# Hybrid RWKV-7 / latent-attention layer on one core: 188 intermediate stores issued by the POOL queue instead of the SP queue

## The chip, the core and the metric

The kernel runs on one core of one Trainium2 chip. A core has TensorE (PE, matrix products; PEld is its weight load), VectorE (DVE), ScalarE (ACT), GpSimd (POOL) and SyncE (SP), each with its own instruction stream that runs in order, and 16 DMA engines that move data between the chip's memory (DRAM) and the on-chip buffer. A DMA is issued by one of the streams: when its turn comes there and its semaphores are met, it is handed to the DMA engines, and the stream goes on. An instruction that waits holds everything behind it in the same stream.

The metric is device time in microseconds. The kernel before ran at a median of 2458.2 us over 3 runs (2451.07 to 2459.61).

## The reference

One decoder layer over 2048 tokens of width 1024. All is float32; the kernel makes each product out of three products of a high and a low part, so every weight is split into two.

```python
u = rmsnorm(h, g_pre)
proj = u @ w_in                                  # 1024 x 5152
feat_a, z_a, c_q, c_kv, k_pe, z_b, gate_logits = split_cols(proj, ...)
f = feat + mu_shift * (prev - feat)              # token shift of r, k, v, wd, ad (1664 columns)
...                                              # branch A: RWKV-7 recurrence over f, group norm, silu(z_a), w_out_a
...                                              # branch B: attention from the latents c_q, c_kv, silu(z_b), w_out_b
gates = sigmoid(gate_logits + b_gate)
merged = g_a * y_a + g_b * y_b
h = h + rmsnorm(merged @ w_o, g_post)
```

## The kernel before, in words

The tokens are cut into four segments of 512 (`NS = 4`), the columns of `w_in` into tiles of 128. There are three phases: projections with the recurrence of branch A (to about 1125 us), attention (to about 1760 us), and the gates, merge and output projection (to the end).

**Projection.** For each column tile `proj` runs 24 matmuls (8 blocks of the contraction, three products each). Its weights come from `load_w` in two halves of four blocks. The first time, a half is loaded raw (`wraw`, two buffers), split by ACT (high part, L247) and POOL (low part, L248) into `whl` (three buffers), and, where the tile is wanted later, stored to DRAM as `d_wi` (L273). Every later time `whl` is loaded ready from `d_wi` (L265). In segment 0 half of the tiles are stored, in segment 1 the other half; in `gates_seg` all 24 tiles are.

**Features.** `proj_seg` shifts r, k, v and the low-rank inputs (`shift`: ACT L328, DVE L330 and L331, a POOL copy of the last column into `halo` at L332) and stores them as `d_k`, `d_r`, `d_v`, `d_wa`; the three latent tiles go out as `d_lat`. `elem` reads these back in halves of a segment (`kf`, `rf`, `vf`, `wat`, and `cum`, `Pi`, `u` for the latents); for segment 0 it does so at once, for the others one to two steps later. `gates_seg` makes 42 tiles of gate factors for the last two segments and stores them as `d_zg`, to be read in the third phase.

**Recurrence.** `step` works on blocks of 256 tokens: `zblock` builds `Zr` and stores it to `d_q`; `gather` reads it back as `Qg` and `Xg`; `invert` runs 30 short DVE steps and stores and reloads the result (`Xinv`); `merge`, `chunk` and `gnorm` follow. These DMAs are on SP (half of the gather on ACT).

**Order.** The program is handed to a scheduler that simulates the engines and puts each engine's instructions, DMA issues among them, in the order of its simulated times. A change of a DMA's queue therefore moves other instructions as well. From the second phase's start on most of the order is fixed by hand (`pin`).

Stores and loads of the first phase are all issued by SP, apart from the loads of `X` from `d_x`, the stores of `d_cq`, `d_kv`, `d_kr` (POOL) and half of the gather (ACT).

Of the kernel before, what the change touches and what calls it, by code (L numbers as in the profile page):

```python
# [21 lines left out]
KC = D // P  # L22
# [18 lines left out]
def f32(ap):  # L41
    return ap.bitcast(F32)
# [7 lines left out]
def hybrid_layer(ctx, tc, x, positions, g_pre, w_in, b_gate, mu_shift, w0, w_decay_up, a0, w_iclr_up, k_k, k_a,  # L50
                 r_k, gn_gain, gn_bias, w_out_a, g_q, w_uq, g_kv, w_ukv, w_out_b, w_o, g_post, out):
    nc = tc.nc
    V, A, G, PE = nc.vector, nc.scalar, nc.gpsimd, nc.tensor
# [14 lines left out]
    sa = pst.enter_context(tc.tile_pool(name="p1a", bufs=1, reuse_waits="tile"))  # L68
# [85 lines left out]
    for name, ap in (("mu", mu_shift), ("w0", w0), ("a0", a0), ("kk", k_k), ("ka", k_a), ("rk", r_k), ("gg", gn_gain),  # L154
                     ("gb", gn_bias), ("gq", g_q), ("gkv", g_kv), ("bg", b_gate)):
        n = ap.shape[0] // P
# [15 lines left out]
    def dcol(o, i=0):  # L172
        return dv[:, o + i:o + i + 1]

    def parameters():

        prow = pp.tile([P, 512], F32, name="prow", tag="z", bufs=2)
        PE.transpose(prow[:, :NR], rows[:NR, :], ident[:NR, :NR])
        A.copy(prm, prow[:, :NR])
        G.tensor_scalar(dv[:, OMU:OMU + 13], cols("mu", 13), -1.0, 1.0, op0=ALU.mult, op1=ALU.add)  # L180
        G.tensor_scalar(dv[:, HW0:HW0 + 4], cols("w0", 4), 0.5, None, op0=ALU.mult)
        G.tensor_scalar(dv[:, HA0:HA0 + 4], cols("a0", 4), 0.5, None, op0=ALU.mult)
        G.tensor_scalar(dv[:, HKA:HKA + 4], cols("ka", 4), 0.5, None, op0=ALU.mult)
        G.tensor_scalar(dv[:, OKA:OKA + 4], cols("ka", 4), -0.5, 1.0, op0=ALU.mult, op1=ALU.add)
        G.tensor_scalar(dv[:, HBG:HBG + 16], cols("bg", 16), 0.5, None, op0=ALU.mult)


    def dtile(name, shape, dt=F32):
        return dr.tile(shape, dt, name=name)

    d_f = {(n, p, s): dtile(f"d_{n}{p}_{s}", [P, 512]) for n in "krv" for p in range(NP) for s in range(NS)}
# [6 lines left out]
    d_wa = {s: dtile(f"d_wa{s}", [P, 512]) for s in range(NS)}  # L198
# [4 lines left out]
    d_zg = {(s, i): dtile(f"d_zg{s}_{i}", [P, 512]) for s, n in ((NS - 1, 24), (NS - 2, 18)) for i in range(n)}  # L203
    d_lat = {(i, s): dtile(f"d_lat{i}_{s}", [P, 512]) for i in range(3) for s in range(NS)}
# [41 lines left out]
    def split(hi, lo, src, ehi, elo):  # L246
        (ehi.copy if ehi is A else ehi.tensor_copy)(hi, src)  # L247
        elo.tensor_tensor(lo, src, f32(hi), op=ALU.subtract)  # L248


    d_w = {}

    def load_w(pool, src, nk, n, elo=None, bufs=3, tag="w", pieces=None, raws=2, key=None, keep=True):


        res = []
        kept = d_w.get(key)
        if key is not None and kept is None and keep:
            d_w[key] = dtile(f"d_w{key}", [P, -(-nk // 4), 2, 4, n])
        for k0 in range(0, nk, 4):  # L260
            m = min(4, nk - k0)
            w = pool.tile([P, 2, m, P], F32R, name=f"{tag}hl", tag=f"{tag}hl", bufs=bufs)
            wn = w if n == P else w[:, :, :, 0:n]
            if kept is not None:
                nc.sync.dma_start(f32(wn), kept[:, k0 // 4])  # L265
            else:
                raw = pool.tile([P, m, P], F32, name=f"{tag}raw", tag=f"{tag}raw", bufs=raws)
                for lo_, n_, ap in (pieces or [(0, n, src)]):
                    nc.sync.dma_start(raw[:, :, lo_:lo_ + n_],
                                      ap[k0 * P:(k0 + m) * P, :].rearrange("(c p) n -> p c n", p=P))  # L270
                split(wn[:, 0], wn[:, 1], raw[:, :, 0:n], A, elo or G)
                if key is not None and keep:
                    nc.sync.dma_start(d_w[key][:, k0 // 4], f32(wn))  # L273
            res += [(w[:, 0, c, 0:n], w[:, 1, c, 0:n]) for c in range(m)]
        return res

# [8 lines left out]
    def proj(ps, w, X, cut=1, mm=PE.matmul):  # L285

        XH, XL = X
        for i in range(cut):
            t = slice(i * 512 // cut, (i + 1) * 512 // cut)
            mm3(ps[:, t], [(w[c], (XH[:, c, t], XL[:, c, t])) for c in range(KC)], mm=mm)  # L290
# [11 lines left out]
    with st:  # L302
# [30 lines left out]
            return f  # L333

        def wtile(c0, n=P, elo=None, keep=True):
            return load_w(sa, w_in[:, c0:c0 + n], KC, n, elo, key=f"i{c0}", keep=keep)

        def pj():
            return ppa.tile([P, 512], F32, name="pj", tag="pj", bufs=2)

        X = [sa.tile([P, KC, 512], F32R, name=n) for n in ("xh", "xl")]
# [87 lines left out]
        def proj_seg(s):  # L429
            make_xT(sa, ppa, "pj", 2, s, g_rep, X)  # L430
            if s == 0:
                parameters()
            cols_ = slice(s * 512, (s + 1) * 512)

            def later(i):

                return bool(s or i % 2)


            ps = pj()  # L440
            proj(ps, wtile(1536, elo=G if s else V, keep=later(0)), X, 2)
            f = shift(ps, 12)
            A.activation(f[0:HD, :], f[0:HD, :], AF.Tanh)
            nc.sync.dma_start(d_wa[s], f)
            yield
            for p in range(NP):
                ps = pj()
                proj(ps, wtile(512 + p * P, keep=later(p)), X)
                f = shift(ps, 4 + p)
                nc.sync.dma_start(d_f["k", p, s], f)  # L450
                yield
            for i, c0 in enumerate((C_CQ, C_CQ + P, C_CKV)):
                ps = pj()
                proj(ps, wtile(c0, keep=later(i)), X)
                f = sa.tile([P, 512], F32, name="lat", tag="fsh", bufs=2)
                A.copy(f, ps)
                nc.sync.dma_start(d_lat[i, s], f)
                yield

            for p in range(NP):  # L460
                for nm, c0, j in (("r", 0, 0), ("v", 1024, 8)):
                    ps = pj()
                    proj(ps, wtile(c0 + p * P, keep=later(j // 8)), X)
                    f = shift(ps, j + p)
                    nc.sync.dma_start(d_f[nm, p, s], f)
                    yield

            ps = pj()
            k1 = w_in[:, C_KPE:C_KPE + 32]
            proj(ps[0:HD, :], load_w(sa, None, KC, HD, pieces=[(0, 32, k1), (32, 16, k1[:, 16:32]),  # L470
                                                               (48, 16, k1[:, 0:16])], key="kpe"), X)
            rt = sa.tile([P, 512], F32, name="rtab", tag="mf", bufs=2)
            nc.sync.dma_start(rt[0:HD], d_rope[32:96, cols_])
            ra = sa.tile([P, 512], F32, name="ra", tag="fsh", bufs=2)
            rb = sa.tile([P, 512], F32, name="rb", tag="fsh", bufs=2)
            V.tensor_tensor(ra[0:32], ps[0:32, :], rt[0:32, :], op=ALU.mult)
            V.tensor_tensor(rb[0:32], ps[32:64, :], rt[32:64, :], op=ALU.mult)
            G.tensor_tensor(ra[0:32], ra[0:32], rb[0:32], op=ALU.add)
            kr = [sa.tile([P, 512], F32R, name=f"kr{k}", tag="mf", bufs=2) for k in range(2)]
            split(kr[0][0:32], kr[1][0:32], ra[0:32], G, G)  # L480
            for k in range(2):
                G.dma_start(d_kr[:, k, cols_], kr[k][0:32])
            yield

        def gates_seg():

            xs = NS - 1
            for s, i in d_zg:
                if s != xs:
                    xs = s  # L490
                    load_xT(X, s)
                ps = pj()
                c0 = (C_ZA, C_ZB, C_G, C_G + 4 * P, C_G + 8 * P, C_G + 12 * P)[i // 4] + (i % 4) * P
                proj(ps, wtile(c0), X)
                th = sa.tile([P, 512], F32, name="thg", tag="mf", bufs=2)
                if i < 8:
                    A.activation(th, ps, AF.Tanh, scale=0.5)
                    V.scalar_tensor_tensor(th, th, 1.0, ps, op0=ALU.add, op1=ALU.mult)
                else:
                    A.activation(th, ps, AF.Tanh, scale=0.5, bias=dcol(HBG, i - 8))  # L500
                nc.sync.dma_start(d_zg[s, i], th)
                yield

        def uv_new():
# [589 lines left out]
    with ExitStack() as st:  # L1094
# [165 lines left out]
        for i in range(NG):  # L1260
# [9 lines left out]
            if i == NG - NS - 1:  # L1270
# [6 lines left out]
                X = [sx.tile([P, KC, 512], F32R, name=n) for n in ("xh3", "xl3")]  # L1277
# [3 lines left out]
        for p in range(4):  # L1281
            if p < 3:
                ps = pp.tile([P, 2, 512], F32, name="pj2", tag="st", bufs=3)[:, 0]
                proj(ps, load_w(sx, w_in[:, C_ZA + p * P:C_ZA + (p + 1) * P], KC, P, elo=V, bufs=5,
                                key=f"i{C_ZA + p * P}"), X, mm=pin)
                th = sx.tile([P, 512], F32, name=f"th0{p}")
# [7 lines left out]
    with ExitStack() as st:  # L1294
# [16 lines left out]
        for si, s in enumerate(order):  # L1311
# [3 lines left out]
            for br, c0, dsrc in ((0, C_ZA, d_ya), (1, C_ZB, d_ob)):  # L1315
                BH = sb.tile([P, NP, 512], F32R, name=f"BH{br}", tag=f"BH{br}", bufs=1)
                BL = sb.tile([P, NP, 512], F32R, name=f"BL{br}", tag=f"BL{br}", bufs=1)
                for p in range(NP):
                    y = t_("yin")
                    nc.sync.dma_start(y, dsrc[p, s])  # L1320
                    th = t_("th3") if s or br or p >= len(gates0) else gates0[p]
# [4 lines left out]
                    else:  # L1326
                        ps = pj()
                        proj(ps, load_w(sx, w_in[:, c0 + p * P:c0 + (p + 1) * P], KC, P, elo=V, bufs=5,
                                        key=f"i{c0 + p * P}"), X)
# [7 lines left out]
            for m in range(KC):  # L1337
                prods = []
                for br, wsrc in ((0, w_out_a), (1, w_out_b)):
# [3 lines left out]
                    else:  # L1343
                        ps = pj()
                        c0 = C_G + br * D + m * P
# [81 lines left out]
```

## Time and profile before

| | before |
|---|---|
| median of 3 runs | 2458.2 us |
| profiled execution | 2459.4 us |
| its span, first to last instruction | 2457.7 us |
| PE / DVE / ACT / POOL busy | 2216.5 / 1099.8 / 710.4 / 1020.3 us |
| DMA moved | 455 MB, 185 GB/s over the span |
| mean granted TensorE clock | 0.950 of full speed |

The span is cut at 145 us (end of segment 0's projections), 720 us (end of segment 3's), 950 us (last weight store), 1125 us (start of the attention phase). The tables of waits name the waiting engine and line, the releaser, the total, the number of waits and the longest. SPq stands for the issues of the SP stream.

### The profile page before, as it was taken

What the parts mean: (1) busy time and instruction counts of PE and PEld (TensorE: products, weight loads), DVE (VectorE), ACT (ScalarE), POOL (GpSimd) and SP (SyncE); (2) the same over time, 40 slices, a digit from 0 to 9 for tenths busy, and PEclk for the clock granted to TensorE, in tenths of its full rate; (3) what the DMA queues carried; (4) which work ended last, traced back from release to release, by engine and by line L of the source; (5) the groups of instructions that cost most, each with busy time, mean ns of one, the idle gap of its engine ahead of it and who ended that gap; (6) DMA issues with size and microseconds to landing.
All of it is one profiled execution on the core that took longest, in us unless ns stands there. A gap on an engine that the chain in (4) does not pass through costs nothing.

```text
span 2457.7 us, 37858 instructions
## 1 busy us (share of the span) xinstructions
PE 2216.5 (90%) x14313; PEld 1646.5 (67%) x14313; DVE 1099.8 (45%) x2007; ACT 710.4 (29%) x1283; POOL 1020.3 (42%) x1194
## 2 busy tenths in 40 slices
PE   7978988988989897998698998988999989999997
PEld 5656776767766675776465655555678867788876
DVE  7155675667475847434353435344230231300312
ACT  4343342333324342123233333332321211111111
POOL 6474443445254655222245653555533232312422
PEclk9989989989999998999699999999999999999999
DMA  7777866647657787574211112050297895766863
GB/s 252 217 251 236 242 211 185 191 125 222 178 174 230 233 239 239 170 230 128 72 58 57 49 59 76 29 189 7 82 371 232 282 325 197 283 204 199 318 245 120
DMA packets 315182, 455.15 MB, mean 185 GB/s; under 512 B 114044, under 2 KB 207288, under 8 KB 309368
## 3 DMA queue, kind: packets, MB, share of 16 engines
q1 hardware_dynamic: 285112, 406.06, 51.3%
q0 software_dynamic: 12608, 42.47, 5.2%
q10 hardware_dynamic: 17280, 4.20, 1.0%
q8 instruction: 113, 1.85, 0.3%
q14 instruction: 69, 0.57, 0.1%
HBM read 313.69 MB, written 132.64 MB: 182 GB/s over the span
## 4 chain that ended last, share of the span: by engine, by line
PE 54%; DMA 18%; DVE 17%; POOL 3%; issue 3%; ACT 2%; SPq 2%; ACTq 0%; DVEq 0%; POOLq 0%
PE pj L281 7%; PE pst L294 7%; PE pj L282 7%; PE pj L283 7%; PE po L294 5%; DMA wraw<-in_w_in_dram 3%; DMA whl<-d_wi 3%; DVE mx L1049 3%; DMA Xg<-d_q 2%; DVE Xg L698 2%; DVE tq L696 2%; PE py L281 2%; PE py L283 2%; PE py L282 2%; PE pq L294 2%
## 5 line engine op out<-in xcount | busy, mean ns | idle before, releaser
L281 PE MATMUL pj<-xh,whl 128*128 128x512 f32 (+1 forms) x1320 | 536.4, 406 | 46.3 <-DMA whl<-d_wi 27.1
L283 PE MATMUL pj<-xh,whl 128*128 128x512 f32 (+1 forms) x1320 | 531.9, 403 | 10.0 <-POOL whl L248 9.7
L282 PE MATMUL pj<-xl,whl 128*128 128x512 f32 (+1 forms) x1320 | 529.9, 401 | 0.0
L1172 POOL TENSOR_TENSOR acc<-acc,pt 128x1024 f32<-128x1024 f32 (+2 forms) x144 | 290.5, 2017 | 204.7 <-PE po L294 177.4
L281 PEld LDWEIGHTS pj<-xh,whl 128*128 128x128 f32 x1320 | 256.2, 194 | 116.6 <-DMA whl<-d_wi 29.6
L283 PEld LDWEIGHTS pj<-xh,whl 128*128 128x128 f32 x1320 | 256.1, 194 | 74.1 <-POOL whl L248 15.3
L282 PEld LDWEIGHTS pj<-xl,whl 128*128 128x128 f32 x1320 | 256.4, 194 | 55.6 <-issue 2.5
L1049 DVE TENSOR_REDUCE mx<-pm 128x2 f32<-128x1024 f32 (+3 forms) x160 | 164.4, 1060 | 148.1 <-PE pm L294 147.4
L248 POOL TENSOR_TENSOR whl<-wraw,whl 128x512 fp32r<-128x512 f32 (+1 forms) x114 | 147.4, 1294 | 160.9 <-ACT whl L247 155.8
L1352 DVE SCALAR_TENSOR_TENSOR tg<-tg,py 128x512 f32<-128x512 f32 x64 | 43.9, 687 | 306.0 <-PE py L283 207.1
L1159 ACT ACTIVATE pt<-pst 128x1024 f32<-128x1024 f32 (+2 forms) x144 | 125.2, 883 | 163.5 <-PE pst L294 150.4
L1354 POOL TENSOR_TENSOR tg<-tg 128x512 f32<-128x512 f32 x32 | 41.2, 1288 | 211.7 <-DVE tg L1352 211.7
L247 ACT CAST whl<-wraw 128x512 fp32r<-128x512 f32 (+1 forms) x116 | 71.1, 615 | 179.4 <-DMA wraw<-in_w_in_dram 106.1
L294 PE MATMUL po<-pt,Vt 128*64 128x512 f32 (+3 forms) x576 | 121.4, 538 | 0.0
L281 PE MATMUL py<-BH,whl 128*128 128x512 f32 x256 | 103.2, 404 | 10.2 <-DMA whl<-d_wo 5.2
L294 PE MATMUL pm<-KH,QH 64*128 64x512 f32 (+3 forms) x312 | 71.6, 447 | 40.5 <-DVE mx L1049 34.8
L282 PE MATMUL py<-BL,whl 128*128 128x512 f32 x256 | 102.8, 402 | 0.0
L283 PE MATMUL py<-BH,whl 128*128 128x512 f32 x256 | 102.6, 402 | 0.0
L696 DVE TENSOR_TENSOR tq<-Xg,Qg 128x30 f32<-128x30 f32 (+7 forms) x240 | 84.8, 353 | 38.4 <-DMA Xg<-d_q 33.0
L282 PE MATMUL pout<-wf,MH 128*128 128x512 f32 x256 | 101.1, 395 | 0.0
L283 PE MATMUL pout<-wf,ML 128*128 128x512 f32 x256 | 99.5, 395 | 0.0
L281 PE MATMUL pout<-wf,MH 128*128 128x512 f32 x256 | 97.3, 395 | 0.1
(368 smaller groups left out, 3953.1 us busy)
## 6 DMA issues: line engine op xcount, KB each, us to landing
whl<-d_wi SPq DMA_DIRECT2D x222, 512.0 KB
d_wi<-whl SPq DMA_DIRECT2D x80, 512.0 KB
wraw<-in_w_in_dram SPq DMA_DIRECT2D x98, 256.0 KB
whl<-d_wo SPq DMA_DIRECT2D x48, 512.0 KB
wf<-d_wf SPq DMA_DIRECT2D x48, 512.0 KB
cqt<-d_cq POOLq DMA_DIRECT2D x16, 1024.0 KB, 5.5
d_zg<-thg SPq DMA_DIRECT2D x42, 256.0 KB
xl<-d_x POOLq DMA_DIRECT2D x8, 1024.0 KB, 9.9
```

Source lines behind the costliest of these rows:

```text
L247: (ehi.copy if ehi is A else ehi.tensor_copy)(hi, src)
L248: elo.tensor_tensor(lo, src, f32(hi), op=ALU.subtract)
L281: mm(ps, lhsT=lh, rhs=rh, start=(i == 0), stop=False)
L282: mm(ps, lhsT=lh, rhs=rl, start=False, stop=False)
L283: mm(ps, lhsT=ll, rhs=rh, start=False, stop=(stop and i == n - 1))
L294: tc.keep_in_program_order(PE.matmul(*args, **kw))
L696: V.tensor_tensor(t3, Xg[:, 0:m, s_:s_ + 1].to_broadcast([P, m, n]), Qg[:, s_:s_ + 1, s_ + 1:32].to_broadcast([P, m, n]), op=ALU.mult)
L698: V.tensor_tensor(Xg[:, 0:m, s_ + 1:32], Xg[:, 0:m, s_ + 1:32], t3, op=ALU.add)
L1049: V.tensor_reduce(mx[:, :, j, c], pm[:, :, 0:w], axis=AX.X, op=ALU.max)
L1159: A.activation(pt[:, :, q0:512], pst[:, :, q0:512], AF.Exp, scale=scale)
L1172: G.tensor_tensor(acc[:, :, q0:512], acc[:, :, q0:512], pt[:, :, q0:512], op=ALU.add)
L1352: V.scalar_tensor_tensor(tg, tg, 1.0, po, op0=ALU.add, op1=ALU.mult)
```

## The change

The 188 stores of the first phase go to POOL's stream: 80 of `d_wi`, 2 of `d_wkpe`, 52 of shifted features, 12 of latents, 42 of gate factors. `load_w` gets an argument `out_q`; its callers in the attention phase and the third phase don't pass it and keep SP. No size, buffer or arithmetic changes.

```diff
-    def load_w(pool, src, nk, n, elo=None, bufs=3, tag="w", pieces=None, raws=2, key=None, keep=True):
+    def load_w(pool, src, nk, n, elo=None, bufs=3, tag="w", pieces=None, raws=2, key=None, keep=True,
+               out_q=None):
...
                 if key is not None and keep:
-                    nc.sync.dma_start(d_w[key][:, k0 // 4], f32(wn))
+                    (out_q or nc.sync).dma_start(d_w[key][:, k0 // 4], f32(wn))
...
         def wtile(c0, n=P, elo=None, keep=True):
-            return load_w(sa, w_in[:, c0:c0 + n], KC, n, elo, key=f"i{c0}", keep=keep)
+            return load_w(sa, w_in[:, c0:c0 + n], KC, n, elo, key=f"i{c0}", keep=keep, out_q=G)
...
-            nc.sync.dma_start(d_wa[s], f)
+            G.dma_start(d_wa[s], f)
...
-                nc.sync.dma_start(d_f["k", p, s], f)
+                G.dma_start(d_f["k", p, s], f)
...
-                nc.sync.dma_start(d_lat[i, s], f)
+                G.dma_start(d_lat[i, s], f)
...
-                    nc.sync.dma_start(d_f[nm, p, s], f)
+                    G.dma_start(d_f[nm, p, s], f)
...
-                                                               (48, 16, k1[:, 0:16])], key="kpe"), X)
+                                                               (48, 16, k1[:, 0:16])], key="kpe", out_q=G), X)
...
-                nc.sync.dma_start(d_zg[s, i], th)
+                G.dma_start(d_zg[s, i], th)
```

The changed file has one line more, so all lines from 254 on read one higher in it. What follows is the order of issues, not times.

SP in segment 0, while the tiles r and v of the first two pairs are projected; before, where `wraw` is a raw weight load, `d_wi` the store of a split half, and `rf`, `vf` the features read back:

```order
L465 DMA d_r_0_268<-fsh 128x512
L269 DMA wraw<-in_w_in_dram 128x4x128
L427 DMA d_rope<-rt 128x512
L578 DMA rf<-d_r_0_268 128x256
L269 DMA wraw<-in_w_in_dram 128x4x128
L465 DMA d_v_0_284<-fsh 128x512
L273 DMA d_wi_1171<-whl 128x1024
L269 DMA wraw<-in_w_in_dram 128x4x128
L578 DMA vf<-d_v_0_284 128x256
L273 DMA d_wi_1171<-whl 128x1024
```

and after:

```order
L531 DMA u<-d_lat_0_410 128x256
L270 DMA wraw<-in_w_in_dram 128x4x128 x3
L579 DMA rf<-d_r_0_268 128x256
L270 DMA wraw<-in_w_in_dram 128x4x128
L579 DMA vf<-d_v_0_284 128x256
L270 DMA wraw<-in_w_in_dram 128x4x128 x3
L579 DMA rf<-d_r_0_272 128x256
```

Only loads are left there; the reads of `d_r` and `d_v` still stand between the raw loads.

POOL at the same place, before (the splits of the weights and the copies into `halo`):

```order
L332 COPY halo<-mf 128x1
L248 TENSOR_TENSOR whl<-wraw,whl 128x512 x2
L332 COPY halo<-mf 128x1
L248 TENSOR_TENSOR whl<-wraw,whl 128x512 x2
L332 COPY halo<-mf 128x1
```

and after:

```order
L248 TENSOR_TENSOR whl<-wraw,whl 128x512
L333 COPY halo<-mf 128x1
L466 DMA d_r_0_268<-fsh 128x512
L248 TENSOR_TENSOR whl<-wraw,whl 128x512 x2
L333 COPY halo<-mf 128x1
L466 DMA d_v_0_284<-fsh 128x512
L274 DMA d_wi_1171<-whl 128x1024
L248 TENSOR_TENSOR whl<-wraw,whl 128x512
L274 DMA d_wi_1171<-whl 128x1024
```

Each feature store stands right behind its `halo` copy, each weight store behind the split of its half.

SP in segment 3, while the k tiles are projected; before (`kf` and `rf` are reads for the recurrence of segment 2):

```order
L265 DMA whl<-d_wi_2474 128x1024
L450 DMA d_k_3_255<-fsh 128x512
L265 DMA whl<-d_wi_2474 128x1024
L265 DMA whl<-d_wi_740 128x1024
L521 DMA kf<-d_k_2_254 128x256
L265 DMA whl<-d_wi_740 128x1024
L450 DMA d_k_3_259<-fsh 128x512
L265 DMA whl<-d_wi_2555 128x1024
L450 DMA d_k_3_263<-fsh 128x512
L578 DMA rf<-d_r_2_278 128x256
L521 DMA kf<-d_k_2_258 128x256
```

and after:

```order
L266 DMA whl<-d_wi_2474 128x1024 x2
L266 DMA whl<-d_wi_740 128x1024 x2
L266 DMA whl<-d_wi_2555 128x1024 x2
L522 DMA kf<-d_k_2_254 128x256
L266 DMA whl<-d_wi_963 128x1024 x2
L266 DMA whl<-d_wi_2628 128x1024
L707 DMA d_q_347<-Xg 1024x1x32
```

The weight loads now stand in pairs, with fewer other issues between them.

## Rows read from the trace of the kernel before

**Rows 1.** Busy time by stage: us, then each engine, PEclk, DMA share, GB/s.

```profile
0.00:145.00 145.00, 119.99 (x511) 90.76 (x512) 64.98 (x127) 57.87 (x103) 82.31 (x191) 0.97 0.76 236
145.00:720.00 575.00, 508.36 (x3914) 390.12 (x3913) 374.77 (x847) 197.29 (x409) 262.24 (x403) 0.92 0.66 199
720.00:950.00 230.00, 203.91 (x1691) 153.96 (x1689) 151.69 (x289) 90.28 (x184) 128.96 (x156) 0.96 0.77 228
950.00:1125.00 175.00, 160.63 (x1351) 125.26 (x1352) 75.23 (x182) 40.82 (x88) 46.04 (x74) 0.94 0.68 209
```

**Rows 2.** Waits of PE, 36 to 145 us: total, times, longest.

```profile
PE pj L281 <- ACT whl L247: 6.3, 4, 2.4
...
PE pj L283 <- POOL whl L248: 1.9, 3, 0.6
```

**Rows 3.** Waits of PE, 145 to 720 us.

```profile
PE pj L281 <- DMA whl<-d_wi: 18.4, 9, 5.8
...
PE pj L283 <- POOL whl L248: 4.8, 1, 4.8
```

**Rows 4.** Waits of PE, 720 to 1125 us.

```profile
PE pj L283 <- POOL whl L248: 3.0, 3, 1.6
...
PE pj L281 <- DMA whl<-d_wi: 2.6, 3, 1.2
...
PE pj L281 <- ACT whl L247: 1.9, 2, 1.0
```

**Rows 5.** Waits of SP's issues, 145 to 720 us.

```profile
SPq L648 <- DVE Zr L644: 52.7, 20, 5.8
SPq L465 <- DVE tq L696: 21.7, 4, 7.2
SPq L465 <- DVE fsh L331: 21.0, 10, 8.1
SPq L815 <- DMA d_ya<-bvb: 18.9, 10, 5.0
SPq L450 <- DVE fsh L331: 15.0, 5, 5.4
SPq L457 <- ACT lat L456: 12.2, 4, 7.6
...
SPq L444 <- ACT rs L757: 8.6, 1, 8.6
```

**Rows 6.** SP's issues in order of time: start, us, line, what.

```profile
580.86 0.32 SPq L265 DMA_DIRECT2D whl<-d_wi  x1
585.28 0.32 SPq L450 DMA_DIRECT2D d_k<-fsh  x1
...
589.52 0.38 SPq L265 DMA_DIRECT2D whl<-d_wi  x1
```

**Rows 7.** Line 273: its issues (ns min/median/max); who waited for them.

```profile
L273 SPq DMA_DIRECT2D d_wi<-whl x80: 319/337/1193, 39.3 to 947.0; - x80
...
  ACT whl L247: 19.3, 5
```

**Rows 8.** DMAs issued by POOL, line 482: ns min/median/max.

```profile
L482 POOL DMA_DIRECT2D d_kr<-kr x8: 517/592/643, 149.1 to 720.7; - x8
```

**Rows 9.** DMAs issued by POOL, line 554: ns min/median/max; us to landing.

```profile
L554 POOL DMA_DIRECT2D d_cq<-lhl x16: 739/811/969, 137.5 to 918.9; - x16
...
DMA to landing us min/median/max: 2.6/4.5/13.1
```

**Rows 10.** Tile fsh: who waited for it.

```profile
  POOL halo L332: 48.9, 17
```

**Rows 11.** Chain that ended last, 36 to 80 us: start, us, what.

```profile
36.59 2.10 DMA d_wa<-fsh
...
76.14 2.06 DMA d_lat<-lat
```

**Rows 12.** The same chain, 40 to 145 us, shares by line.

```profile
by line: DMA wraw<-in_w_in_dram 51.9%; POOL whl L248 13.1%; DMA d_cq<-lhl 7.2%; ACT whl L247 6.4%; issue 5.0%; PE pj L283 4.4%; PE pj L281 4.3%; PE pj L282 3.7%; SPq L273 2.3%; DMA wat<-d_wa 2.1%; DMA d_lat<-lat 2.0%; SPq L269 1.4%; ACT lat
```

## Prediction

> **What bounds the kernel now.** I read the busy time by stage first. All moved stores lie before 1125 us, so only the first four stages can change directly. There PE is busy 119.99 of 145 us, 508.36 of 575, 203.91 of 230 and 160.63 of 175 [rows 1]: 992.9 of 1125, so 132.1 us of idle PE is all that a better order of DMAs could win in work of this size. DMA engines are busy 66 to 77%, so a store that changes its queue still competes with the loads for the same engines. POOL is busy 57, 46, 56 and 26% of the four stages [rows 1]: there is room for more, but in segment 0 and in the stage to 950 us not much.
>
> Second I read what PE waits for, since only a part of its idle time is about weights. It waits for ready weight loads 18.4 us [rows 3] and 2.6 us [rows 4], 21.0 together; for ACT's cast, which is late when the raw load was late, 6.3 us [rows 2] and 1.9 [rows 4], 8.2 together; for POOL's split 1.9 [rows 2], 4.8 [rows 3] and 3.0 [rows 4], 9.7 together. That is 38.9 us. The rest of the 132.1 us is the start, the recurrence's chain through DVE, and the seams between segments, where the change has no store.
>
> Third, what holds the loads back on SP. In 145 to 720 us the issues that are to leave SP waited 21.7 + 21.0 (r and v), 15.0 (k), 12.2 (latents) and 8.6 us (wa), 78.5 us in these five rows. Issues that stay there waited 52.7 us for `Zr` and 18.9 us for `d_ya`, 71.6 us [rows 5]. While SP waits, all loads behind stand still. One place shows it: a weight load goes out at 580.86, then a store of `d_k` only at 585.28, and the next weight load at 589.52 [rows 6]. From the end of the first issue to the store, 4.1 us, SP stood before a store that now leaves; the rest up to the load is a read of `kf` that stays, and its wait.
>
> **What is removed.** 188 issues leave SP, 0.337 us each at the median of the weight stores [rows 7], 63 us of SP issue time, and with them their waits. I give the loads the share of SP's waits that leaves: 78.5 of 78.5 + 71.6, 52%. Of the 21.0 us for ready weights and 8.2 us for raw loads that is 0.52 x 29.2 = 15.2 us of PE idle time gone. Its ends: 0, if the waits that stay simply take over (the load at 589.52 would then still stand behind the read of `kf`); and 29.2 us, if every load is early enough. I take the middle since the order after has the weight loads of segment 3 in pairs, but with the `kf` reads and the gather still between some of them.
>
> **What is added on POOL.** 32 issues before 145 us (14 weight halves, 16 features and latents, 2 of kpe), 66 to 720 us (48 and 18), 90 after that (48 halves, 42 gate tiles). The trace of before shows POOL issuing no store of these shapes. The nearest rows are `d_kr` with 0.592 us and `d_cq` with 0.811 us at the median, 0.517 and 0.969 at the ends [rows 8, 9]. I take 0.592, since a weight store has one unbroken run per partition and `d_cq` has two; 188 x 0.592 = 111 us of POOL, and 97 to 182 us by the ends. Most of it lies in gaps: a weight store comes right behind the split that made it, where POOL waits for the next cast, and a feature store right behind the `halo` copy, which already waits for the same DVE instruction (48.9 us in 17 waits [rows 10]), so it adds no wait of its own. What is on the path is a split that finds an issue ahead of it. Segment 0 has 32 x 0.592 = 19 us of issues in some 109 us (from 36 us on), 17%, and the stage to 950 us some 72 x 0.592 = 43 us in 230, 19%. With about 30 and 48 splits, half an issue of delay each time: 78 x 0.18 x 0.3 = 4.2 us. If no gap covered any of it, the two stages would pay 19 + 43 = 62 us; if all were covered, nothing. I take 4.2, since PE's waits for splits are only 9.7 us now.
>
> The gate stores are a new wait on POOL: each waits for ACT (for the first eight tiles of a segment, DVE after it), and the split of the tile after next and the recurrence's small operations queue behind it. The split of the tile after next needs a `whl` buffer that the same projection releases, so it could not have started much earlier; I count it as nothing. If that cover is gone, the split starts later by one issue, 0.592 us, and by what ACT and DVE need for the gate tile, once per tile.
>
> **The sum.** 2459.4 (the profiled execution, of which 2457.7 is span) - 15.2 + 4.2 = 2448.4 us. The median of the runs shown is 1.2 us below the profiled time, so 2447 us. Own range: from -29.2 (2430) to no gain and the split term doubled, 2459.4 - 1.2 + 8.4, cut at 2460. A measurement of this kernel can tell about 0.5% from no change, 12.3 us: 2446 to 2470 counts as the same. The forecast lies on the lower edge of that.
>
> **Rival 1: no change, because other waits hold the loads.** SP keeps the waits for `Zr` and `d_ya` (71.6 us) and its waits for PE to free `whl`; the loads then go out when they did. For it: between 580.86 and 589.52 only 4.1 of 8.3 us belong to a moved store. Against it: the pairs in the order. Price: 0 - (-4.2): 2458 + 4 = 2462 at worst, 2458 as I set it.
> The Trainium skill, "DMA: Bandwidth & Descriptors", section "Issuing engines are not separate DMA queues", says that DMAs from all streams end on the same 16 engines and that a second issuer saves only sequencer time, usually little beside the transfer. By that rule this rival is the result; that the waits in SP's order, and not its issue time, hold the loads is what the trace has to set against it.
>
> **Rival 2: slower, through the features that are read back at once.** In segment 0 all 16 feature and latent stores are read back immediately, and these reads still stand between the raw weight loads on SP. On SP's queue such a store landed in 2.10 and 2.06 us [rows 11]; a store that POOL issues, of the same 256 KB, landed in 4.5 us at the median and 13.1 at most [rows 9]. That is 2.4 us more for each of 16 reads, 38 us in which SP stands before a read, and raw loads behind it are 51.9% of the chain there [rows 12]: 20 us. From the point where the store has to wait behind POOL's splits as well it grows. The later landing also keeps the three `whl` buffers: ACT already waited 19.3 us in 5 waits for a store to leave [rows 7], 3.9 us each; two more of them cost 8. Without the gain of the forecast: 2458 + 20 + 4 + 2 = 2484. For it: the landing times. Against it: SP has fewer issues, and so reaches reads later than the wait needs; and in segments 1 to 3 the reads come a step later.
>
> **Rival 3: the whole wait for weights goes, and the recurrence's DMAs come sooner.** All 29.2 us, and of the waits around `Zr` (52.7 us of SP) a fifth, some 10 us: 2420 us. For it: SP was the stream with most waits. Against it: DVE, not SP, ends those.
>
> **Rival 4: POOL's issues are held by DVE.** If DVE's work held POOL's issue, each could take as much longer as the longest row is above the shortest, 0.969 - 0.517 = 0.45 us, times the 104 issues of segment 0 and the stage to 950 us = 47 us more on POOL where splits feed PE: 2505. Against it: DVE is busy 45 and 66% of these stages [rows 1], and no issue in the 24 of the two rows took over 0.969 us.
> The Trainium skill, "SBUF — State Buffer", section "SBUF: two separate sides", says that a DMA from POOL's queue cannot write its descriptors while DVE runs an instruction that takes both of its ports, and a later section gives 620 ns alone and some 3100 ns overlapped; 2.5 us on 188 issues would be 466 us of POOL, as an estimate from that page. The rows with their 0.969 us at most speak against it here.
>
> **How the numbers follow.** Forecast 0.50, rival 1 0.12, rival 2 0.23, rival 3 0.12, rival 4 0.03. Likeliest time 2447. For 8 in 10 I leave out the lower part of rival 3 and the upper part of rivals 2 and 4: 2424 to 2484. Faster than 2446: a little under half of the forecast and rival 3, 0.24 + 0.12 = 0.36. Slower than 2470: rival 4 and nearly all of rival 2, 0.03 + 0.21 = 0.24. Same: what is left of the forecast and rival 2, and rival 1, 0.26 + 0.02 + 0.12 = 0.40.
>
> **What would show it.** Right: PE's waits for `whl<-d_wi` in 145 to 720 us fall from 18.4 to about 9 us; SP's largest waits are those for PE, `Zr` and `d_ya`; POOL issues take about 0.6 us; POOL's busy time grows by about 111 us; PE's waits for POOL's split stay under 15 us. Wrong: SP's reads of `d_r`, `d_v`, `d_lat` waiting for stores by tens of us in segment 0 (rival 2); POOL issues of several us (rival 4); or a change of the same size in the phases after 1125 us, where no store changed its queue.

## Result and profile after

The changed kernel takes 2494.1 us (median of 5 runs, 2488.98 to 2499.99), the kernel before 2457.2 beside it (5 runs): ratio 1.0153, 95% interval 1.0138 to 1.0169. It is 37 us slower; the forecast was 2447, with a range that ended at 2484. The profiled span is 2492.0 us.

Busy time by stage of the kernel after, with the columns of [rows 1]:

```profile
0.00:145.00 145.00, 118.55 (x511) 90.05 (x511) 64.21 (x126) 58.26 (x104) 97.06 (x221) 0.98 0.71 225
145.00:720.00 575.00, 504.08 (x3916) 386.26 (x3916) 389.73 (x847) 196.58 (x409) 297.11 (x472) 0.92 0.68 203
720.00:950.00 230.00, 196.66 (x1632) 148.55 (x1633) 139.08 (x276) 85.07 (x176) 153.40 (x213) 0.92 0.67 204
950.00:1125.00 175.00, 149.62 (x1328) 117.64 (x1328) 78.73 (x194) 43.80 (x94) 64.88 (x102) 0.93 0.71 209
```

To 720 us PE does nearly what it did in [rows 1] (508.36 there in the second stage). From 720 to 1125 us it is busy 346.3 us where it was 364.5: 18 us more of idle time, and PE's granted clock is lower at first (0.92 against 0.96). The loss is here, where the gate factors are computed beside the last steps of the recurrence. The activation of the first gate factor starts at 722.8 us (721.4 before), that of the last at 1151.2 (1122.6). The attention phase begins behind the last one, and its last matmul comes 636 us later in both traces: of the 37 us, 28.6 stand in this one number. Another 5 us are behind the attention phase (704.5 us to the end, 699.2 before), where no store changed its queue; what makes them was not looked into.

The lines that the prediction asked for came out as it said, but for one of SP's. PE's wait for ready weight loads, 145 to 720 us, against 18.4 in [rows 3]:

```profile
PE pj L282 <- DMA whl<-d_wi: 8.4, 4, 5.1
```

POOL's issues (ns min/median/max) of the weight halves, with their landing in us, and of the gate factors:

```profile
L274 POOL DMA_DIRECT2D d_wi<-whl x80: 531/567/648, 40.8 to 987.7; - x80
...
DMA to landing us min/median/max: 2.9/4.6/7.5
```

```profile
L502 POOL DMA_DIRECT2D d_zg<-thg x42: 539/581/654, 727.6 to 1152.2; - x42
```

And SP's largest waits, 145 to 720 us, where [rows 5] had the stores' waits for DVE and ACT:

```profile
SPq L266 <- PE pj L284: 116.1, 47, 5.4
SPq L649 <- DVE Zr L645: 49.0, 20, 4.6
SPq L270 <- POOL whl L248: 24.6, 8, 7.3
```

(The third is a wait for POOL's splits, where the forecast had `d_ya`.) The largest of them, for PE to free a buffer of `whl`, was SP's largest before as well, and smaller:

```profile
SPq L265 <- PE pj L283: 67.0, 31, 5.7
```

So SP is rid of the stores' waits, PE waits 10 us less for weights, POOL's busy time grew by 95.5 us (forecast 111): the rows look like the mechanism, and the kernel is slower all the same. SP doesn't wait less in all: its waits of these 575 us add up to 401 us, 369 before. The experiments had to find what the forecast had no term for.

### The profile page after: what moved, and what is told of

It reads as the page before. It is cut to its first block, busy times and chain, and to the rows that moved or that the text cites. A ratio compares the mean times of both kernels' runs of the same rounds, so it can differ in the third digit from the quotient of the medians.

```text
span 2492.0 us, 37866 instructions
## 1 busy us (share of the span) xinstructions
PE 2215.2 (89%) x14313; PEld 1648.2 (66%) x14313; DVE 1105.3 (44%) x2007; ACT 710.1 (28%) x1283; POOL 1115.8 (45%) x1382
## 5 line engine op out<-in xcount | busy, mean ns | idle before, releaser
L283 PE MATMUL pj<-xl,whl 128*128 128x512 f32 (+1 forms) x1320 | 524.6, 397 | 0.0
L295 PE MATMUL pm<-KH,QH 64*128 64x512 f32 (+3 forms) x312 | 72.0, 447 | 39.7 <-DVE mx L1050 34.0
```

Source lines behind the costliest of these rows:

```text
L283: mm(ps, lhsT=lh, rhs=rl, start=False, stop=False)
L295: tc.keep_in_program_order(PE.matmul(*args, **kw))
```

## Experiments

Three theories were held against each other. **Theory 1 (queue, POOL)**: the issues and their waits crowd POOL. **Theory 2 (queue, SP)**: SP, rid of the stores, runs ahead and its transfers get in the way. **Theory 3 (order)**: the queue matters little, but the scheduler, which sees other costs, puts the other instructions in another order. All ratios are to the kernel before in the same comparison, with 95% intervals. "First" and "last" are the starts of the first and the last gate factor's activation (721.4 and 1122.6 before).

### Parts of the change

Each kernel passes `G` at some of the changed places only (98 stores of segments, 48 weight halves and 42 factors of the gate stage; e9_wa moves four stores and nothing else):

```diff
# e1_zg: 42 gate factors
-  nc.sync.dma_start(d_zg[s, i], th)
+  G.dma_start(d_zg[s, i], th)
# e9_wa: 4 stores of d_wa
-  nc.sync.dma_start(d_wa[s], f)
+  G.dma_start(d_wa[s], f)
```

| run | on POOL | us | ratio (interval) | first, last |
|---|---|---|---|---|
| e1_zg | gate factors | 2443.1 | 0.9955 (0.9935 to 0.9974) | 718.5, 1107.4 |
| e4_seg | segments' stores | 2445.8 | 0.9966 (0.9949 to 0.9983) | 723.7, 1109.9 |
| e3_wg | gate stage's weights | 2469.6 | 1.0059 (1.0043 to 1.0076) | 719.9, 1141.9 |
| e2_allbutzg | all but gate factors | 2456.6 | 0.9997 (0.9982 to 1.0012) | 721.8, 1125.1 |
| e5_gates | gate stage's weights and factors | 2487.1 | 1.0134 (1.0115 to 1.0153) | 720.7, 1162.9 |
| e11_segzg | segments and gate factors | 2454.2 | 0.9991 (0.9975 to 1.0006) | 722.0, 1123.3 |
| e9_wa | 4 stores of d_wa | 2486.1 | 1.0124 (1.0108 to 1.0140) | 740.3, 1154.7 |
| e6_zgact | as the change, factors on ACT | 2456.8 | 1.0009 (0.9994 to 1.0024) | 725.5, 1123.9 |

Expected of e1_zg: 

> Of the 188 stores only the 42 of the gate factors go to POOL, all others stay on SP. Theory 1 (POOL's queue is too crowded in the gate stage, 720 to 1010 us: recurrence operations and weight splits stand behind stores there; cost grows with the number of issues on POOL in that stage, 72 before 950 us in the change): these bring about a third of the issues of that stage, so +8 to +15 us over the kernel before. Theory 2 (SP, freed of stores, runs ahead to reads of features that wait for a buffer, and raw weight loads stand behind them): SP still has the weight stores between them, so 0 to +8 us. Theory 3 (no cause in the queues: the scheduler makes another order and this one is unlucky): any value from -25 to +40 us, with no relation to the parts.

Expected of e2_allbutzg: 

> All stores of the change but the 42 gate factors go to POOL (146 of 188). Theory 1: two thirds of the issues of the gate stage stay on POOL, +20 to +28 us over the kernel before. If the gate factors' own wait on POOL is what costs, 0 to +8 us. Theory 2: SP is nearly as free as in the change, +20 to +37 us. Theory 3: any value from -25 to +40 us.

Expected of e3_wg: 

> Only the 48 weight stores of the gate stage go to POOL. Theory 1: about half of the cost of the change, +12 to +20 us. Theory 2: SP loses the stores that stand between its raw loads, +15 to +30 us. Theory 3: any value from -25 to +40 us.

Expected of e4_seg: 

> Only the stores of the four segments go to POOL (32 weight halves, 2 of kpe, 64 features and latents); the gate stage is as before. In the changed kernel the gate stage began 3 us later than before (first gate store at 727.6 against 724.6 us), so by theories 1 and 2 the time is -5 to +8 us from the kernel before. Theory 3: any value from -25 to +40 us.

Expected of e5_gates: 

> The 48 weight stores and the 42 gate factors of the gate stage go to POOL, the stores of the segments stay on SP. So far, against the kernel before: the gate factors alone gave -11 us, these weight stores alone +14 us, the stores of the segments alone -9 us, all 188 +37 us. If the two classes of the gate stage spoil each other on POOL (theory 1: a queue that holds both, at 90 issues, is too full), +40 to +50 us. If effects simply add, +3 us. Theory 3 (order by chance): no relation.

Expected of e11_segzg: 

> All stores of the change but the 48 weight stores of the gate stage go to POOL; those stay on SP. If the parts add, -11 - 9 = -20 us against the kernel before, about 2437 us, and the weight stores of the gate stage are the part that turns the change slow (theory 1 by their place between the splits; theory 2 since with them SP keeps its pace). Theory 3: anything, such as +10 us.

Expected of e6_zgact: 

> As the change, but the 42 gate factors go to the ACT queue instead of POOL's. SP is as free of stores as in the change, POOL holds as much as in the run that left the gate factors on SP (+1 us). Theory 2 (SP without stores runs ahead to reads that block its raw loads): +25 to +40 us, as the change. Theory 1 (POOL too full): -5 to +10 us. Theory 3: no relation.

Expected of e9_wa: 

> Only the four stores of the low-rank inputs (d_wa) go to POOL, one per segment: too few to load any queue. By theories 1 and 2 the time stays within 4 us of the kernel before. Theory 3 (the scheduler's order by chance carries effects of ten and more us): as much as 8 to 20 us of difference in either direction.

What follows. The three disjoint parts make -11 (e1), -8 (e4) and +14 us (e3) by their ratios, some -5 together; the whole makes +37. The pairs don't add either: e5_gates makes +33 where the parts add to +3 and theory 1 had 40 to 50, e11_segzg -2 where they add to -20, e2_allbutzg -1 where theories 1 and 2 had +20 or more (0 to 8, if the gate factors' own wait was to blame). In e6_zgact SP is as free as in the change, and the loss is gone: SP's freedom does not bring the loss by itself (the order is another one there too). In e9_wa SP keeps 184 of the 188 stores and POOL has four issues more, and it loses 31 us, 19 of them before the first gate factor; no price per store gives that. Where it loses, PE idles and its granted clock is lower. Before and e9_wa, 480 to 560 us (columns as above):

```profile
480.00:560.00 80.00, 71.13 (x742) 54.04 (x740) 56.21 (x119) 32.39 (x68) 36.58 (x56) 0.91 0.52 142
```

```profile
480.00:560.00 80.00, 63.06 (x581) 47.98 (x580) 60.52 (x138) 26.73 (x58) 35.59 (x58) 0.81 0.45 134
```

### A collision at the segment's reload, and a control that kept the order

A fourth theory came from the slow traces. Between the factors of segment 3 and of segment 2 POOL loads segment 2's transposed inputs, four loads of 1 MB, and in the slow kernels these go out together with the recurrence's short reload of its inverse. DVE's wait for it, 940 to 1020 us, in e3_wg and in e9_wa (total, times, longest):

```profile
DVE XT L719 <- DMA Xinv<-d_q: 16.3, 2, 15.5
```

```profile
DVE XT L719 <- DMA Xinv<-d_q: 11.2, 2, 10.9
```

In the changed kernel itself this wait is 4.0 us, but DVE waits 6.6 us more for another short reload, of `bvb`, that went out behind the first two of the loads (before: no wait for either near this place, where its four loads go out 9.7 us and more ahead of the reload). Start, us, what, idle time before:

```profile
975.86 0.70 DVE L720 STREAM_TRANSPOSE XT<-Xinv 32x512 f32<-32x512 f32 x1 [3.06 <-DMA Xinv<-d_q]
...
978.41 0.70 DVE L720 STREAM_TRANSPOSE XT<-Xinv 32x512 f32<-32x512 f32 x1 [0.92 <-DMA Xinv<-d_q]
985.70 0.48 DVE L817 SCALAR_TENSOR_TENSOR bvb<-ypt,prm,bvb 128x256 f32<-128x256 f32 x1 [6.58 <-DMA bvb<-d_ya]
```

xa_nox and xb_nox are the kernels after and before without these four loads (they leave the segment's reload out); na_pool and nb_pool have a dummy of one column on POOL in each segment instead, meant to shake the order:

```diff
# xa_nox, xb_nox (in gates_seg)
-                if s != xs:
-                    xs = s
-                    load_xT(X, s)
# na_pool, nb_pool (in proj_seg)
+            G.memset(nul, 0.0)
```

Expected of xa_nox: 

> The changed kernel without the reload of the transposed segments in the gate stage (left out: the gate factors of segments 2, 1 and 0 are then computed from segment 3's X; 12 loads of 1 MB go). Collision theory: no wait of DVE for Xinv or bvb above 4 us near 970, and 10 to 20 us less than the changed kernel, 2474 to 2484. Queue theory: 2488 to 2494, since 12 loads less free POOL of 12 issues only, and the gates stay late. Order theory: anything in 2440 to 2494, since the order moves as well.

Expected of xb_nox: 

> The kernel before without those 12 loads (same part left out). Collision theory: the kernel before has its X loads 9 us ahead of the Xinv reload and waits little there: 0 to 5 us less, 2452 to 2458. Queue theory: 2457, within 3 us. Order theory: anything in 2440 to 2480.

Measured: xa_nox 2474.3 (1.0089, 1.0065 to 1.0113), xb_nox 2437.7 (0.9943, 0.9929 to 0.9958). (The expectation of xa_nox counts loads of three segments; the gate stage has only segment 2's four, and its 18 gate factors come from segment 3's inputs here.) By the ratios after gains 16 us (20 by the medians, as expected), but before gains 14, where 0 to 5 were expected. Without the loads the two are still 36 us apart: the collision is not the whole difference between them, and the theory falls as the cause of the 37. The order moved in both as well, so the gains are not the loads' alone, and how much of the changed kernel's loss is the 10.6 us above stays open.

Expected of na_pool: 

> The changed kernel with one dummy memset of one column on POOL per segment's projection (4 in all, nothing reads it). No store changes its queue against the changed kernel; the instruction order moves. Queue theory (POOL's crowding, or SP freed): as the changed kernel, 2494, within 5 us. Order theory (the time hangs on where the order happens to put loads): off 2494 by more than 8 us, either way; if it is an ordinary draw, between 2443 and 2480. Collision theory within it: if the four X loads of segment 2 (L245) are issued at least 8 us before the Xinv reload near 970, then under 2480; if within 3 us of it, 2485 to 2500.

Expected of nb_pool: 

> The kernel before with the same four dummy memsets; all stores stay on SP. Queue theory: 2457, within 3 us. Order theory: off 2457 by more than 5 us, somewhere in 2443 to 2490. Collision theory: 2440 to 2460 if the X loads are issued at least 8 us before the Xinv reload near 970, above 2470 if not.

Measured: na_pool 2493.0 (1.0165, 1.0149 to 1.0182), nb_pool 2456.7 (1.0005, 0.9992 to 1.0018). Taken as written, this is for the queue theory. But the dummies left every other instruction of all five engines in its place in both kernels, apart from some 20 of POOL's set-up operations before 35 us, so the order was not shaken and the two theories were not told apart. They show something else: with the order kept, the time stays within a few us.

### The order held, the queue changed

A scheduled program can be held to a list: after the program is traced, each instruction gets an edge of order (no semaphore) to the one that stands ahead of it on its engine in the list. So the queue of one kernel can run in the order of the other:

```diff
     with tile.TileContext(nc, schedule_with_timeline_sim=True) as tc:
         hybrid_layer(tc, *args)
+        pin(tc, nc)    # for each engine: tc.add_manual_dep(i, previous.name, NoSync)
```

PE, DVE and ACT then have their instructions in exactly the listed order; only the 188 stores change their row. No run holds a kernel to its own list, so what the holding costs by itself is not shown (the last run of this section, with the order of e1_zg and another queue, comes within 1 us of it).

Expected of p_bq: 

> The changed kernel (all 188 stores on POOL) with every engine's instructions held to the order of the kernel before, which is written down as a list; each store stands in POOL's row where it stood among all instructions before. Order theory: within 8 us of the kernel before, 2449 to 2465. Queue theory (the issues on POOL, or SP freed of them, cost the time by themselves): 2485 to 2500. Between the two, 2466 to 2484: both, and the share of each is read from it.

Expected of p_aq: 

> The kernel before (all 188 stores on SP) held to the order of the changed kernel in the same way. Order theory: 2485 to 2500, the loss without the change of queue. Queue theory: 2449 to 2465. Between: both.

| order of | stores on SP | stores on POOL |
|---|---|---|
| before | 2457 us; gate stage 721.4 to 1122.6 | p_bq 2473.0, 1.0066 (1.0043 to 1.0089); 725.9 to 1137.0 |
| after | p_aq 2482.4, 1.0104 (1.0083 to 1.0126); 715.0 to 1145.9 | 2494, 1.0153 (1.0138 to 1.0169); 722.8 to 1151.2 |

Both have a share, and they nearly add: order 26 us with the stores on SP and 21 with them on POOL, queue 16 in the order of before and 12 in its own (by the ratios, at 2457). The gate stage is 401.2 us long before, 430.9 in p_aq: the order alone makes it 29.7 us longer, while it brings the first gate factor 6.4 us forward. With the order the same, start times can be compared instruction by instruction. With the stores on POOL, DVE's instructions start later by a median (of those within 10 us) of 1.5 us at 130 us, 6.7 at 300, 4.6 at 720, 18.4 at 980 and 14.7 at 1130 in the order of before; by 1.5, 7.9, 9.0, 5.6 and 5.3 in the order of after. So the queue costs some 5 to 9 us in the segments, mostly by 300 us; in the gate stage it costs 10 more in an order that was not made for it, and nothing in one that was. (In the order of after that is 5 of the 12 us; of the rest 3 come behind the gate stage in the two traces, and the traced run of p_aq was its slowest, 3 us above its median.)

What POOL's issues do to the order of before is seen in PE's waits for the split, 720 to 1000 us, before and p_bq, and in p_bq's POOL, which stands before a gate store until ACT or DVE has made the tile:

```profile
PE pj L283 <- POOL whl L248: 3.0, 3, 1.6
```

```profile
PE pj L284 <- POOL whl L248: 10.2, 5, 4.4
```

```profile
POOL d_zg L502 <- ACT thg L501: 5.0, 1, 5.0
POOL d_zg L502 <- DVE thg L499: 3.7, 3, 2.2
```

In the segments the queue's cost shows on SP, at the reads of features that were stored just before. Its waits for these stores to land, 36 to 145 us, add up to 19.0 us before and 39.7 in p_bq, 8.6 in p_aq and 26.4 after.

The same pairs take the credit for the weight loads from the queue. PE's waits for ready weights, 145 to 720 us, in p_bq (stores on POOL) and in p_aq (stores on SP):

```profile
PE pj L282 <- DMA whl<-d_wi: 22.1, 12, 6.9
```

```profile
PE pj L281 <- DMA whl<-d_wi: 8.9, 4, 6.0
```

18.4 fell to 8.4 with the new order, whichever queue has the stores; with the order kept the queue alone brought nothing (18.4 to 22.1, 8.9 to 8.4).

The next three runs have the stores on POOL and an order that goes over from one kernel's to the other's: p_h1 from before's to after's at the first gate factor, p_h2 the other way round there, p_h3 from after's to before's at the 22nd.

Expected of p_h1: 

> The changed kernel, stores on POOL, held to the order of before up to the first gate factor (near 720) and to its own order for everything after. If the order of the gate stage costs the time: 2485 to 2500, with the X loads of segment 2 within 3 us of the Xinv reload. If the order ahead of 720 does: 2449 to 2465. Queue theory: 2485 to 2500 too, so it is told from that by the next run.

Expected of p_h2: 

> The other half: the changed kernel, stores on POOL, in its own order up to the first gate factor and in the order of before after it. Gate stage's order theory: 2449 to 2465, X loads well ahead of the Xinv reload. Order ahead of 720: 2485 to 2500. Queue theory: 2485 to 2500.

Expected of p_h3: 

> The changed kernel, stores on POOL, in its own order through the activation of the 22nd gate factor (near 955), then in the order of before. In its own order 128 matmuls of the recurrence stand in PE's row between the 24th and the 25th gate factor, in the order of before 35; the two earlier long stretches of its own order (100 ahead of the 5th, 90 ahead of the 15th) stay. If the long stretches cost the time and the last one most: 2472 to 2483, the last gate factor near 1139. If the loss is made before 955: 2488 to 2500. If it is spread over all three: 2483 to 2488.

Measured: p_h1 2508.5 (1.0211, 1.0190 to 1.0232), p_h2 2473.8 (1.0074, 1.0049 to 1.0100), p_h3 2471.4 (1.0065, 1.0038 to 1.0092). With after's order in the gate stage the loss is there, with before's only 16 to 18 us of it are left, the queue's share, whatever the order ahead of it. (p_h1 was expected at 2485 to 2500. It loses 14 us at its seam, where the one order goes over to the other: up to there it runs within 3 us of p_bq, but three more instructions of ACT stand ahead of the first gate factor's activation, 740.0 us against 725.9. From the first to the last factor it takes 426.0 us, the changed kernel 428.4, p_h2 409.5, p_h3 and p_bq 411.1.) And p_h3 places the loss, for stores on POOL: after's order costs nothing that can be measured up to the 22nd factor, all of it comes behind. From the activation of the 22nd factor to that of the last, behind the same instructions, it is 195.9 us in after's order and 175.9 in before's. p_h3, p_h2 and p_bq agree within 2.5 us.

Counted in the program, 8 other matmuls stand in PE's row of before between the 23rd and the 24th gate factor, 35 ahead of the last of the 25th; after the change 56 and 128. The new order puts most of a step of the recurrence, whose matmuls wait for DVE again and again, ahead of the 25th factor, and that one waits for the reload of segment 2's inputs besides (its loads go out at 975.9 to 994.7 us). After (start, us, what, idle time before):

```profile
974.96 0.60 PE L679 MATMUL pv<-ident,vf 128*128 128x128 f32 x4
975.80 0.66 PE L679 MATMUL pv<-ident,vf 128*128 128x128 f32 x4 [0.24 <-ACT BT L672]
987.51 1.91 PE L725 MATMUL pf<-XT,Zr 32*32 32x32 f32 x64 [11.05 <-DVE uv L687]
```

The same place in p_h3:

```profile
983.33 1.06 PE L679 MATMUL pv<-ident,vf 128*128 128x128 f32 x4
984.36 0.79 PE L282 MATMUL pj<-xh,whl 128*128 128x512 f32 x1
...
994.12 0.40 PE L284 MATMUL pj<-xh,whl 128*128 128x512 f32 x1
994.45 1.59 PE L725 MATMUL pf<-XT,Zr 32*32 32x32 f32 x64
```

In p_h3 the matmuls of the 25th gate factor and the first half of the 26th (`pj`) fill the 10 us from `pv` to `pf`; in the changed kernel PE stands idle there. These 11 us are DVE's waits for the two reloads shown above, 10.6 us. In p_aq, with the same order, DVE waits 8.5 us for them and PE stands idle for 3.9 and 3.2 us, and the gate stage is as long (430.9): this one gap is an example, not the sum. Busy time and clock in 945 to 1015 us, before, after, p_h3:

```profile
945.00:1015.00 70.00, 58.38 (x486) 45.08 (x486) 40.07 (x83) 15.68 (x35) 25.45 (x36) 0.90 0.70 222
```

```profile
945.00:1015.00 70.00, 50.06 (x461) 39.26 (x463) 41.93 (x92) 17.88 (x40) 39.34 (x58) 0.83 0.67 214
```

```profile
945.00:1015.00 70.00, 55.91 (x385) 42.79 (x384) 47.78 (x94) 18.10 (x37) 41.53 (x60) 0.88 0.77 255
```

PE is busy 8.3 us less than before in these 70, and at a lower granted clock. The recurrence itself gains by it (its last `Y` is read at 1143.8 us after the change, 1155.5 in p_h3), but that doesn't help: the attention phase starts behind the last gate factor (1151.2 and 1134.8), and the recurrence's tail runs beside it.

What the order changes over the whole stage is DVE's waits for the recurrence's short reloads (`Xg`, `bvb`, `Xinv`), from the first to the last gate factor: 24.6 us before, 22.9 in p_bq and 26.7 in p_h2; 45.5 in p_aq, 50.3 after and 48.1 in p_h1; 37.5 in p_h3. With after's order it is 20 to 27 us more, whichever queue has the stores.

Neither these waits nor long stretches are a measure across all kernels: e3_wg waits 60.4 us and loses 14, and e11_segzg has 135 other matmuls ahead of the last of its 25th factor and loses nothing. So where the loss arises is shown, behind the 22nd factor with the stores on POOL; by which step of the recurrence is in part argued.

Last, whether the gain of e1_zg is the order's too: p_1q is the kernel before, all stores on SP, in e1_zg's order.

Expected of p_1q: 

> The kernel before, all 188 stores on SP, held to the order of the kernel with only the gate factors on POOL (e1_zg, 2443, 12 us under before). Order theory: that gain is the order's as well, 2440 to 2449. Queue theory (42 stores less on SP make the gain): 2452 to 2460.

Measured: 2444.0 (0.9965, 0.9949 to 0.9981), e1_zg 2443.1. The gain needs no store on POOL: it is the order's. e1_zg is the fastest of the kernels that leave nothing out, 12 us under before.

## Why the prediction was wrong

**The failed step is the sum.** "2459.4 - 15.2 + 4.2" has a term for the queue and one for the loads, and none for the order of the gate stage. I read the new order at one place, for the weight loads of segment 3 ("I take the middle since the order after has the weight loads of segment 3 in pairs"), and took the rest of PE's row as unchanged. It was not: that row is reordered from segment 0 on, and in the gate stage this alone costs 29.7 us (p_aq); with the stores on POOL all that can be measured of it comes behind the 22nd factor (p_h3). What the sum did price failed as well: the queue alone, -11 us in it, costs 16 us in before's order and 12 in after's.

**The -15.2 us.** The wait fell to 8.4 us where about 9 was forecast, but not by the cause given: with before's order and the stores on POOL it is 22.1, with after's order and the stores on SP 8.9. And it bought little: the first gate factor comes 6.4 us sooner in p_aq, of which the queue takes 7.8 back (715.0 to 722.8). The size of the row was right by luck, its cause and its worth were not. The 52% behind it was read off a part of SP's waits: it leaves out the largest, 67.0 us for PE to free `whl`. Of all of them, 369 us, the stores' are 111, 30%, and the same rule would have given 9 us. (The row of `Zr` in [rows 5] covers 200 to 720 us; from 145 it is 54.3.) Even that would not have come: in before's order SP waits 404 us with the stores gone, since the waits that stay take over.

**The splits, +4.2 us.** In segment 0 to 145 us PE's waits for splits went from 1.9 to 4.0 us in before's order and from 3.6 to 5.7 in after's, 2.1 each: the mechanism holds. But the whole queue share of the segments is 4.6 to 7.8 us at the first gate factor. Another part is features' stores: DVE's buffer for the rotation waited 3.6 us for a store of `d_v` to leave in p_bq (0.4 before), and SP waited 18 to 21 us longer for the stores whose features it reads back. As a price of the queue the term was too small by a factor of three to four (16 and 12 us).

**The gate stores, "I count it as nothing".** Right in after's own order (gate stage 428.4 on POOL, 430.9 on SP), wrong in before's (411.1 against 401.2), where splits stand behind stores that wait (7 of the 10 us are PE's waits for splits, 10.2 against 3.0). The step priced a store in an order that would no longer be there.

**The issue time.** 0.567 and 0.581 us against 0.592, POOL's busy time +95.5 us against +111: right.

**The rivals.** Rival 2 named the nearest time, 2484 (its sum adds 2 us for the `whl` buffers where its text has 8). Its mechanism is real and small: the order hides it, since the segments ended only 1.4 us later (722.8 against 721.4), but with the order held they end 4.6 and 7.8 us later, and SP's waits for the stores that it reads back, up to 145 us, grow by 21 and 18 us. That the total came near was luck. Rival 3 is out: no kernel with all the stores on POOL came under 2471. Rival 4 is out, since no store's issue took over 0.933 us. The Trainium skill, "SBUF — State Buffer", section "A bandwidth-pool intuition that's wrong (but worth ruling out)", has a DMA of such a queue at some 3100 ns where it overlaps with a copy on DVE, against 620 ns alone; these issues show no such step. Rival 1 took the change for neutral; that the waits which stay take over is seen, 369 us of SP's waits before and 401 after. The Trainium skill, "DMA: Bandwidth & Descriptors", section "Issuing engines are not separate DMA queues", allows a second issuer no more than sequencer time; with the order held the second issuer gained nothing here, and cost 16 and 12 us. No rival had the order as its mechanism, and "what would make it wrong" looked at segment 0, the issues and the phases behind 1125 us, not at the stretch between.

## What to carry to other kernels

Where a scheduler sets the order, a change of queue is two changes, and the order can be the larger: price it at the seams, by what stands in PE's row while the slow chain (here DVE's) runs, and ask whether independent matmuls are there to fill it. To tell the two apart, hold one kernel to the other's order; parts of a change that don't add up, or four stores that cost 31 us, say that this is needed. A row that moves as forecast is no proof of its cause until the other half of the change is held still.

## Not expected of the hardware

- A short reload of the inverse, issued together with four loads of 1 MB from another queue, kept DVE waiting up to 10.9 and 15.5 us (e9_wa, e3_wg); in xa_nox, without these loads (and in another order), the longest such wait there was 1.8 us.
- The matmul of 512 columns that took 0.39 us took 0.63 behind the 11 us gap of the changed kernel, at a granted clock of 0.53 from 987 to 993 us, near the lower of the two levels (1.2 GHz); from 993 to 1000 it was 1.00 again. So a gap is paid partly a second time, behind it. The short ones are as well: before, the same matmul took 0.63 us from 968.9 to 972 us, at 0.50, behind waits of 3.3 and 4.3 us.
- With the order kept, four more instructions left the time where it was (2456.7 and 2493.0 against 2454 to 2457 and 2494): differences of ten and more us between the variants are not scatter.
